# State space output with channels on partitions, and a written order of four engines for groups 2 to 7

## The chip, the cores and the metric

The kernel runs on one core of a Trainium2 chip. Its time is the device time of one execution in microseconds; less is better. The core has TensorE for matrix products (in the profile PE, and PEld for its loading of weights), VectorE (DVE), ScalarE (ACT), GpSimd (POOL) and SyncE (SP), which here issues most of the DMAs that bring the weights in.

## The reference, cut to what matters

The program is one inference step of a streaming encoder: a Mamba-2 mixer, a block of looked-up experts ("peer"), attention, a second peer block and a last norm. The change lies in the mixer, which works on 384 tokens of width 1024: 256 of one prompt and 8 samples of 16 tokens that continue stored states.

```python
def mamba_mixer(xn, ssm_prev, conv_prev, w_in, conv_w, conv_b, dt_bias, a_log, d_skip, norm_g, w_out):
    proj = xn @ w_in
    z, xbc, dt_raw = ...                       # 2048 gates, 2048 x + 1024 B + 1024 C, 32 heads
    xbc, conv_new = causal_conv(xbc, conv_prev, conv_w, conv_b)   # 4 taps in time, then silu
    ...
    dt = softplus(dt_raw + dt_bias)
    y, s_new = ssd_scan(xs, dt, A, Bm, Cm, ssm_prev, ...)
    y = y + xs * d_skip[:, None]               # the skip
    y = y * silu(z)                            # the gate
    y = rmsnorm(y, norm_g)
    return y @ w_out, s_new, conv_new

# in ssd_scan, for each block of tokens i, j, each head r with 64 channels p:
xdt = x * dt
cb = einsum('bcign,bcjgn->bcijg', C, B)
y_diag = einsum('bcijgr,bcjgrp->bcigrp', cb * lmat, xdt)               # inner products
states = einsum('bcjgn,bcjgrp->bcgrpn', B, xdt * decay_end)            # new states
y_off = einsum('bcign,bcgrpn->bcigrp', C, s_prev) * exp(acum)          # products with the old states
y = y_diag + y_off
```

The 32 heads form 8 groups of four; a group shares B and C. A group has 256 channels of x and of z, and 128 each of B and C.

## The kernel before, in words

The tokens lie in three blocks of 128 (NB = 3): two of the prompt and one of all the samples. The normed input is kept with its 1024 features on partitions, split into a high and a low part (xhi, xlo), and so is every weight tile after its load: raw (a DMA of 512 KB on SP's queue), hi (ScalarE, line 132) and lo = raw - hi (VectorE, line 133). A product in full precision is then three matmuls for each of 8 slices of features: hi by xhi, hi by xlo, lo by xhi (lines 168 to 170). 24 such matmuls of 128 columns of weights by 384 tokens are called a tile here.

A group has six pieces of weight: a B tile, a C tile, two x tiles (x0, x1) and two of the gate. The first four end in a convolution (`conv_tile`): GpSimd puts the stored tokens at the head (lines 396, 397), ScalarE evicts the product into xp, GpSimd copies the last tokens out (lines 400, 401), ScalarE makes the first tap, VectorE the other three (line 406), and ScalarE applies silu. These results have channels on partitions. `gate` makes z with tokens on partitions (72 matmuls of 256 columns, lines 460 to 462). `decay` makes ab, a matrix of 128 by 128 tokens for every head and block: the decays (line 473, twelve instructions), an exponential on ScalarE, and the product with C by B (cb). `tokens` transposes x and scales it by dt (xdt) and by dt and the decay to the block's end (xde, line 498).

`states` (line 506) makes the new prompt states. `outputs` computes a group's y with tokens on partitions, in banks of PSUM:

```python
pe.matmul(o[:, j * P:(j + 1) * P], self.xs[:, j, b * P:(b + 1) * P], self.dg[:, j], ...)   # skip, L518
pe.matmul(o[:, cs], self.ab[:, rr, b], self.xdt[:, b, cs], ...)                            # inner, L522
```

Here dg is a diagonal matrix of the skip's weights, which GpSimd makes anew for each group (line 432). The products with the old states (lines 525, 529) stand in a bank of their own, pO; VectorE fades them, adds the rest and multiplies with the gate (lines 534 to 538). ScalarE squares y and sums it over channels into a column of ssq for each block and group. `turn` transposes y (line 547) and splits it into yhi and ylo, the operands of the output projection. `carry` makes the new sample states: it fades s0 (line 553), and eight products (line 561) are added to it.

The program loops over the groups. In loop g stand the tiles of group g and, between them, the steps of the group before: `states` and `outputs` behind the B tile, `turn` behind C, `carry` behind x0. How the instructions come to stand in each engine's queue is decided by a scheduler when the program is built; only where `pin` or `in_order` is used (nowhere in this loop but for the eight products of `carry` and two copies) does the queue keep the order of the code. Group 7's outputs, turn and carry stand in the output projection (`out_terms`, whose sixteen terms are w_out's row blocks). PSUM is used through a ring of eight banks, which are given out in the order of the code.

Of the kernel before, what the change touches and what calls it, by code (L numbers as in the profile page):

```python
# [19 lines left out]
P = 128  # L20
# [48 lines left out]
def encoder_step(ctx: ExitStack, tc: tile.TileContext, t_in, t_out):  # L69
# [165 lines left out]
    def mamba(h_src):  # L235
        with ExitStack() as c:
# [62 lines left out]
            ssq = T(one, [P, NB, GROUPS], F32, tag="ssq")  # L299
# [11 lines left out]
            if True:  # L311
# [77 lines left out]

                def conv_tile(ci, out):  # L390
# [3 lines left out]
                    xp = T(two, [P, XPW], F32, tag="xp")  # L394
                    xs_ = xp[:, PADP:].rearrange("p (s w) -> p s w", w=SEG)
                    pool.memset(xp[:, 0:3], 0.0)
                    pool.tensor_copy(xs_[:, :, 0:3], sconv[:, ci])
                    act.copy(xp[:, 3:PADP], ps[:, :NP])
                    act.copy(xs_[:, :, 3:], ps[:, NP:].rearrange("p (s w) -> p s w", w=TS))
                    pool.tensor_copy(cst[:, ci, 0], xp[:, NP:PADP])  # L400
                    pool.tensor_copy(cst[:, ci, 1:], xs_[:, :, TS:])
                    cv = T(two, [P, XPW], F32, tag="cv")
                    act.activation(cv[:, :CVW], xp[:, 0:CVW], AF.Identity, scale=convw[:, ci, 0:1],
                                   bias=convb[:, ci:ci + 1])
                    for k in range(1, 4):
                        dve.scalar_tensor_tensor(cv[:, :CVW], xp[:, k:k + CVW], convw[:, ci, k:k + 1], cv[:, :CVW],
                                                 op0=OP.mult, op1=OP.add)
                    act.activation(out[:, :NP], cv[:, :NP], AF.Silu)
                    act.activation(out[:, NP:].rearrange("p (s w) -> p s w", w=TS),
                                   cv[:, PADP:].rearrange("p (s w) -> p s w", w=SEG)[:, :, :TS], AF.Silu)  # L410
# [4 lines left out]
                class Group:  # L415


                    def __init__(self, g):
                        self.g = g
                        self.hs = slice(4 * g, 4 * g + 4)  # L420

                    def fetch(self):
                        g = self.g
# [3 lines left out]
                                                        ap=[[0, P], [1, 4 * NB * P]]))  # L427
# [1326 lines left out]
```

## Time and profile before

| what | value |
|---|---|
| time of three runs | 2357.51, 2357.73, 2358.8 us; median 2357.73 |
| the profiled execution | 2358.57 us, its span 2356.7 us, mean granted TensorE clock 0.996 |
| PE, busy share of the span | 2306.2 us, 98% |
| PEld | 1979.3 us, 84% |
| DVE | 1964.8 us, 83% |
| ACT | 1251.5 us, 53% |
| POOL | 764.1 us, 32% |
| the first state product (line 506) of each group | 100.18, 135.68, 171.00, 206.31, 241.62, 277.00 us for groups 1 to 6 |
| start of the output projection | 307.87 us |

Times are in microseconds from the span's start, "xN" counts instructions, and "out<-in" gives the tiles that an instruction writes and reads, with buffer numbers left out. Engines overlap, so their busy times do not add up to the span. The mixer takes the first 387 us or so; the steady part of the loop over groups runs from 100 to 308 us.

### The profile page before, as it was taken

The numbers are of one execution on the slowest core, as the hardware profiler recorded it, in microseconds if no ns is written. First come the engines' busy times: TensorE is split into PE (matmuls) and PEld (weight loads), VectorE is DVE, ScalarE is ACT, GpSimd is POOL, SyncE is SP. The second block draws the span as 40 slices with busy tenths as digits, with TensorE's granted clock in tenths as the row PEclk, the third lists the DMA queues.
The fourth block names the chain that finished last, engine by engine and source line by source line (L and its number), as shares of the span: only waits on it lengthen the run. The fifth ranks groups of instructions, "written<-read, shape, count | busy, mean of one in ns | idle before, by whom it ended". The sixth has DMA issues, their size and how long they took to land. (4 is left out here: it accounts for less than half of the span.)

```text
span 2356.7 us, 44413 instructions
## 1 busy us (share of the span) xinstructions
PE 2306.2 (98%) x16606; PEld 1979.3 (84%) x16607; DVE 1964.8 (83%) x4227; ACT 1251.5 (53%) x2428; POOL 764.1 (32%) x779
## 2 busy tenths in 40 slices
PE   7999999999999999999999999999999999999998
PEld 7899987999999997667776787999999997667775
DVE  5888855979998999888876676979988999898876
ACT  5666534344476676554444555344466666554443
POOL 2323200002154333555563200011144324555562
PEclk9999999999999999999999999999999999999999
DMA  5554435357699889999997515367699889999997
GB/s 189 190 188 170 155 128 185 117 193 246 239 358 334 327 298 333 381 372 387 403 419 295 166 64 181 117 206 258 234 356 333 312 306 334 384 367 391 409 419 282
DMA packets 177944, 649.76 MB, mean 276 GB/s; under 512 B 21232, under 2 KB 23136, under 8 KB 175328
## 3 DMA queue, kind: packets, MB, share of 16 engines
q1 hardware_dynamic: 100800, 365.85, 42.6%
q0 software_dynamic: 76928, 281.07, 31.9%
q8 instruction: 130, 2.13, 0.4%
q14 instruction: 86, 0.70, 0.1%
HBM read 630.62 MB, written 18.06 MB: 275 GB/s over the span
## 5 line engine op out<-in xcount | busy, mean ns | idle before, releaser
L132 ACT CAST hi<-raw 128x1024 fp32r<-128x1024 f32 (+1 forms) x475 | 495.4, 1043 | 666.1 <-PE bank L169 322.6
L133 DVE TENSOR_TENSOR lo<-raw,hi 128x1024 fp32r<-128x1024 f32 (+1 forms) x475 | 575.8, 1212 | 197.7 <-ACT hi L132 196.9
L1250 POOL DMA_INDIRECT gath<-in_p_u,eidU x226 | 288.5, 1276 | 831.7 <-DVE gath L1299 514.9
L168 PE MATMUL bank<-xhi,hi 128*128 128x256 f32 (+1 forms) x1344 | 400.9, 299 | 0.0
L170 PE MATMUL bank<-xhi,lo 128*128 128x256 f32 (+1 forms) x1344 | 393.3, 293 | 5.3 <-DVE lo L133 5.1
L169 PE MATMUL bank<-xlo,hi 128*128 128x256 f32 (+1 forms) x1344 | 392.3, 292 | 0.0
L168 PEld LDWEIGHTS bank<-xhi,hi 128*128 128x128 f32 x1344 | 253.6, 189 | 12.7 <-issue 8.9
L170 PEld LDWEIGHTS bank<-xhi,lo 128*128 128x128 f32 x1344 | 253.3, 188 | 8.2 <-DVE lo L133 8.0
L169 PEld LDWEIGHTS bank<-xlo,hi 128*128 128x128 f32 x1344 | 253.5, 189 | 0.8 <-issue 0.2
L1250 POOL DMA_INDIRECT G<-in_p_v,eidT x192 | 223.8, 1166 | 78.5 <-issue 53.3
L168 PE MATMUL bank<-qhi,hi 128*128 128x256 f32 (+1 forms) x784 | 232.7, 297 | 0.0
L170 PE MATMUL bank<-qhi,lo 128*128 128x256 f32 (+1 forms) x784 | 227.4, 290 | 2.2 <-DVE lo L133 2.2
L169 PE MATMUL bank<-qlo,hi 128*128 128x256 f32 (+1 forms) x784 | 228.4, 291 | 0.0
L1413 ACT ACTIVATE oa<-ioh,e2T 128x128 f16<-128x128 f16 x512 | 163.3, 391 | 96.3 <-PE bank L1425 96.3
L183 PE MATMUL bank<-hi,phi 128*128 128x512 f32 x632 | 206.1, 405 | 1.5 <-ACT phi L132 1.5
L132 ACT CAST hix<-raw 128x1024 fp32r<-128x1024 f32 x118 | 123.9, 1050 | 152.3 <-PE bank L183 69.8
L183 PE MATMUL bank<-lo,phi 128*128 128x512 f32 x632 | 197.7, 392 | 0.9 <-DVE lo L133 0.9
L183 PE MATMUL bank<-hi,plo 128*128 128x512 f32 x632 | 196.4, 390 | 0.0
L133 DVE TENSOR_TENSOR lox<-raw,hix 128x1024 fp32r<-128x1024 f32 x118 | 143.9, 1220 | 22.2 <-ACT hix L132 21.9
L183 PEld LDWEIGHTS bank<-hi,phi 128*128 128x128 f32 x632 | 113.6, 188 | 49.5 <-ACT phi L132 19.1
L170 PEld LDWEIGHTS bank<-qhi,lo 128*128 128x128 f32 x784 | 147.9, 189 | 2.6 <-DVE lo L133 2.6
L169 PEld LDWEIGHTS bank<-qlo,hi 128*128 128x128 f32 x784 | 148.9, 190 | 0.4
(395 smaller groups left out, 5173.1 us busy)
## 6 DMA issues: line engine op xcount, KB each, us to landing
raw<-in_u_t SPq DMA_DIRECT2D x256, 512.0 KB
raw<-in_p_v SPq DMA_DIRECT2D x256, 512.0 KB
raw<-in_w_in SPq DMA_DIRECT2D x32, 512.0 KB
raw<-in_p_w_q SPq DMA_DIRECT2D x32, 512.0 KB
raw<-in_w_z SPq DMA_DIRECT2D x16, 512.0 KB
s<-in_state_ssm SPq DMA_DIRECT2D x8, 1024.0 KB
out_sm_ssm<-s SPq DMA_DIRECT2D x8, 1024.0 KB
raw<-in_w_out SPq DMA_DIRECT2D x16, 512.0 KB
```

The costliest lines, as they stand in the source:

```text
L132: act.copy(hi, raw)
L133: dve.tensor_tensor(lo, raw, hi32, op=OP.subtract)
L168: pe.matmul(ps, whi[:, s], xhi[:, k, c0:c1], start=(k == 0), stop=False)
L169: pe.matmul(ps, whi[:, s], xlo[:, k, c0:c1], start=False, stop=False)
L170: pe.matmul(ps, wlo[:, s], xhi[:, k, c0:c1], start=False, stop=(k == KD - 1))
L183: mm = pe.matmul(halves[hf], x, w[:, hf * n:(hf + 1) * n], start=s_, stop=e_)
L1250: pool.indirect_dma_start(out=tile_, out_offset=None, in_=tab, in_offset=bass.IndirectOffsetOnAxis(ap=idx, axis=0))
L1413: act.activation(a[:, i], ioh, AF.Square, scale=-1.0, bias=e2T[:, t, 0:1])
```

## The change

The mixer's y is now computed with channels on partitions, and the loop is rewritten.

- Inner products: xdt's 64 channels of a head are the stationary operand and ab the moving one, so that a matmul writes 64 partitions by 128 tokens; two heads share a bank, one in its lower and one in its upper half. Skip and gate are applied by VectorE (`gated`), and dg is gone. The gate is two ordinary tiles, with w_z laid out as the other weights are.
- The products with the old states keep their form; faded (yo), they are transposed and added by four matmuls with the identity (`add_outer`).
- y needs no transpose before its split (`turn`). The squares are summed over groups by GpSimd (`squares`), and over channels at the end by three matmuls with a column of ones.
- Groups 0 and 1 are left to the scheduler. For groups 2 to 7 one loop over 36 tiles stands in `in_order` with GpSimd added, so that PE, DVE, ACT and POOL keep the order of the code. Each tile runs its 16 matmuls with high weights and then the 8 with low weights; the raw weights are loaded two tiles ahead; the steps of the group before stand at fixed tiles: its state products inside the B tile, its four new-state pairs (`s0_products`, "four quarters") after x1. The loop also splits the first two blocks of w_out.
- The last `else` of the loop is reached for x0 as well as for z1, so `x_turn` stands twice in a group: behind x0, where its target px is written again later without having been read, and behind z1.

```diff
-                        pY = [bank([P, 256]), bank([P, 2, 256])]
-                        for b in range(NB):
-                            o = pY[0] if b == 0 else pY[1][:, b - 1]
-                            for j in range(2):
-                                pe.matmul(o[:, j * P:(j + 1) * P], self.xs[:, j, b * P:(b + 1) * P], self.dg[:, j],
-                                          start=True, stop=False)
...
+                    def inner(self, j):
+                        self.pY[j] = bank([P, NT])
+                        for b in range(NB):
+                            for r in range(2):
+                                cs = slice(64 * (2 * j + r), 64 * (2 * j + r) + 64)
+                                pe.matmul(self.pY[j][64 * r:64 * r + 64, b * P:(b + 1) * P], self.xdt[:, b, cs],
+                                          self.ab[:, 2 * j + r, b], start=(b == 0), stop=False)
...
-                        dve.tensor_tensor(y[:, 0], self.zs[:, 0], pY[0], op=OP.mult)
-                        dve.tensor_tensor(y[:, 1:], y[:, 1:], pY[1], op=OP.add)
-                        dve.tensor_tensor(y[:, 1:], y[:, 1:], self.zs[:, 1:], op=OP.mult)
-                        for b in range(NB):
-                            act.activation(self.zs[:, b], y[:, b], AF.Square, accum_out=ssq[:, b, g:g + 1])
+                    def add_outer(self):
+                        for j in range(2):
+                            for b in (1, 2):
+                                pe.matmul(self.pY[j][:, b * P:(b + 1) * P], self.yo[:, b - 1, j * P:(j + 1) * P], ident,
+                                          start=False, stop=(b == 2))
...
+                    def gated(self, j):
...
+                        dve.scalar_tensor_tensor(y[:, j], self.xs[:, j], dsk[:, c:c + 1], self.pY[j],
+                                                 op0=OP.mult, op1=OP.add)
+                        dve.tensor_tensor(y[:, j], y[:, j], self.zs[:, j], op=OP.mult)
+
+                    def squares(self, j):
+                        if self.g == 0 and j == 0:
+                            act.activation(ssq, self.y[:, j], AF.Square)
+                        else:
+                            act.activation(self.zs[:, j], self.y[:, j], AF.Square)
+                            pool.tensor_tensor(ssq, ssq, self.zs[:, j], op=OP.add)
...
-                            pt = bank([P, NT])
-                            for b in range(NB):
-                                pe.transpose(pt[:, b * P:(b + 1) * P], self.y[:, b, j * P:(j + 1) * P], ident)
-                            split(yhi[:, ct], ylo[:, ct], pt, scale=ng[:, ct:ct + 1])
+                            split(yhi[:, ct], ylo[:, ct], self.y[:, j], scale=ng[:, ct:ct + 1])
...
+                with in_order(HELD + (mybir.EngineType.Pool,)):
+                    for i, (g, k) in enumerate(tiles):
...
+                        act.copy(nhi, raw)
+                        if pend and pend[0]:
+                            pend[0].evict(pend[2])
+                        elif pend:
+                            act.activation(pend[1], pend[2], AF.Silu)
+                        if k == "b":
+                            if g > 2:
+                                for b in range(NB):
+                                    p.x_scale(b)
+                            p.state_products()
...
+                        if k == "c":
+                            p.state_sum()
+                            p.fade_outer()
+                        dve.tensor_tensor(nlo, raw, nhi.bitcast(F32), op=OP.subtract)
+                        wt = nhi, nlo
+                        if pend and pend[0]:
+                            pend[0].sum()
+                        if k == "b":
+                            c.spans(range(2 if g > 2 else 0, 4))
+                        elif k == "c":
+                            p.s0_fade()
+                        elif k == "x0":
+                            for j in range(2):
+                                p.gated(j)
+                        elif k == "x1":
+                            for j in range(2):
+                                p.squares(j)
+                            p.turn()
+                        elif k == "z0":
+                            p.s0_sum()
+                        elif k == "z1":
+                            p.store()
+                            c.weigh()
+                            if nx:
+                                nx.spans(range(2))
...
+                        if k == "b":
+                            p.inner(0)
+                            p.outer()
+                            p.inner(1)
+                        elif k == "c":
+                            p.add_outer()
+                        elif k == "x1":
+                            p.s0_products(range(4))
+                        elif k == "z0":
+                            c.pairs()
+                            c.b_turn()
+                        else:
+                            for b in range(NB):
+                                c.x_turn(b)
...
-                dve.tensor_reduce(ry, ssq, axis=AX.X, op=OP.add)
-                dve.tensor_scalar(ry, ry, 1.0 / INNER, EPS, op0=OP.mult, op1=OP.add)
+                dve.tensor_scalar(ry, psq[0], 1.0 / INNER, EPS, op0=OP.mult, op1=OP.add)
```

Where the rows stand now is shown at four places (a row is line, operation, tile written, tiles read, shape written). First TensorE's queue at the outputs of one group, before (three more pairs that read like the second one stand behind it and are left out):

```order
L518 MATMUL bank_2336<-dg_1924,xs_2032 128x128
L522 MATMUL bank_2336<-xdt_2259,ab_1920 128x64 x2
L518 MATMUL bank_2337<-dg_1924,xs_2032 128x128
L522 MATMUL bank_2337<-xdt_2259,ab_1920 128x64 x2
L518 MATMUL bank_2337<-dg_1924,xs_2032 128x128
L522 MATMUL bank_2337<-xdt_2259,ab_1920 128x64 x2
L525 MATMUL bank_2356<-st_2329,CT_1972 128x256
L529 MATMUL bank_2356<-s_318_1922,cm_59_252 32x256 x8
```

And the same place now (bank_2513 is the next group's B tile, bank_2593 its C tile):

```order
L704 MATMUL bank_2513<-xlo_108,hi_2478 128x384
L546 MATMUL bank_2545<-xde_2537,Bt_2500 128x256 x2
L724 MATMUL bank_2513<-xhi_107,lo_2479 128x384 x8
L564 MATMUL bank_2569<-ab_1981,xdt_2536 64x128 x6
L569 MATMUL bank_2576<-st_2544,CT_2267 128x256
L573 MATMUL bank_2576<-s_384_2237,cm_61_256 32x256 x8
L564 MATMUL bank_2586<-ab_1981,xdt_2536 64x128 x6
L703 MATMUL bank_2593<-xhi_107,hi_2532 128x384
```

Six skip and twelve inner products became twelve inner products of another shape, and the two state products moved into the B tile, ahead of its eight low-weight matmuls. Next TensorE's queue behind the x0 tile, now:

```order
L704 MATMUL bank_2650<-xlo_108,hi_2614 128x384
L724 MATMUL bank_2650<-xhi_107,lo_2615 128x384 x8
L527 MATMUL bank_2703<-ident_69,xs_2699 128x128 x2
L527 MATMUL bank_2706<-ident_69,xs_2699 128x128 x2
L527 MATMUL bank_2709<-ident_69,xs_2699 128x128 x2
L703 MATMUL bank_2712<-xhi_107,hi_2669 128x384
```

Six transposes of xs stand between x0 and x1, where the queue had none. VectorE's queue from the products with the old states of one group on, before:

```order
L534 TENSOR_TENSOR y_2768<-bank_2758,etok_245 128x512
L553 TENSOR_TENSOR s_378_2324<-s_378_2324,decS_247 128x2048
L537 TENSOR_TENSOR y_2768<-y_2768,bank_2739 128x512
L473 SCALAR_TENSOR_TENSOR ab_3126<-ab_3126,acum_243,msk_251 128x128 x12
L538 TENSOR_TENSOR y_2768<-y_2768,zs_2655 128x512
L133 TENSOR_TENSOR lo_2903<-raw_2900,hi_2902 128x1024
```

And VectorE's queue now, from the gating of a group's y on:

```order
L604 SCALAR_TENSOR_TENSOR y_2690<-xs_2324,dsk_236,bank_2586 128x384
L606 TENSOR_TENSOR y_2690<-y_2690,zs_2450 128x384
L728 TENSOR_TENSOR lo_2734<-raw_2667,hi_2733 128x1024
L414 SCALAR_TENSOR_TENSOR cv_2740<-xp_2700,convw_223,cv_2740 128x408 x3
L136 SCALAR_TENSOR_TENSOR ylo_238<-y_2690,ng_234,yhi_239 128x384 x2
L728 TENSOR_TENSOR lo_2799<-raw_2729,hi_2798 128x1024
L414 SCALAR_TENSOR_TENSOR cv_2805<-xp_2764,convw_223,cv_2805 128x408 x3
```

The twelve decays no longer stand in one piece between two steps of y; a tile's low weights (lo), the convolution of the tile before it and one step of the earlier group follow one another. Last GpSimd's queue, before:

```order
L396 MEMSET xp_1602 128x3
L397 COPY xp_1602<-sconv_227 128x8x3
L400 COPY cst_229<-xp_1504 128x3
L401 COPY cst_229<-xp_1504 128x24
L432 TENSOR_SCALAR dg_1522<-ident_69,dsk_236 128x128 x2
```

And now (zs holds the squares):

```order
L405 COPY cst_229<-xp_1200 128x3
L406 COPY cst_229<-xp_1200 128x24
L613 TENSOR_TENSOR ssq_246<-ssq_246,zs_920 128x384 x2
L398 MEMSET xp_1264 128x3
L399 COPY xp_1264<-sconv_227 128x8x3
```

The two instructions that made dg are gone, and two additions of the squares stand ahead of the memset and copy that open the next convolution.

More of the change, by code (lines that the diff above doesn't have):

```diff
@@ L393, in conv_tile @@
                     gemm_cols(ps, split_raw(early.pop(ci, None) or load_raw(t_in["w_in"][ci])), xhi, xlo, 0, NT)
[L394 to L410, printed above, removed]
+                    t = Conv(ci)
+                    t.evict(ps)
+                    t.sum()
+                    t.silu(out)
                 def heads(ap):
@@ new lines, in b_turn, with b_keep @@
+                    def b_turn(self):
+                        self.pb = bank([P, NB, P])
+                        for b in range(NB):
+                            pe.transpose(self.pb[:, b], self.BT[:, b * P:(b + 1) * P], ident)
+                    def b_keep(self):
+                        self.Bt = Bt = T(two, [P, 4, P], F32, tag="Bt", bufs=1)
+                        act.copy(Bt[:, 0:2], self.pb[:, 0:2])
+                        for w in range(2):
+                            act.activation(Bt[:, 2 + w], self.pb[:, 2], AF.Copy, scale=parm[:, w:w + 1])
@@ L525, in outputs, with outer @@
+                    def outer(self):
+                        self.pO = pO = bank([P, 2, 256])
                         pe.matmul(pO[:, 0], self.CT[:, P:2 * P], self.st[:, 0], start=True, stop=True)
@@ new lines, in mamba @@
+                gs = [Group(g) for g in range(GROUPS)]
+                g0, g1 = gs[:2]
+                st_ = steps()
+                g0.b_tile()
+                g0.c_tile()
+                next(st_)
+                g0.x_tile(0)
+                g0.x_tile(1)
+                g0.gate()
+                next(st_, None)
+                g0.fetch()
+                g0.tokens()
+                g1.b_tile()
+                g1.c_tile()
+                g1.fetch()
+                g1.x_tile(0)
+                g0.decay()
@@ new lines, in mamba, with source @@
+                g0.states()
+                g0.outputs()
+                g1.x_tile(1)
+                g0.finish()
+                g0.carry()
+                g1.decay()
+                g0.turn()
+                g1.gate()
+                g0.store()
+                g1.tokens()
+                tiles = [(g, k) for g in range(2, GROUPS) for k in ("b", "c", "x0", "x1", "z0", "z1")]
+                def source(g, k):
+                    if k[0] == "z":
+                        return t_in["w_z"][g, int(k[1])]
+                    return t_in["w_in"][{"b": 16 + g, "c": 24 + g, "x0": 2 * g, "x1": 2 * g + 1}[k]]
@@ L625, in out_terms @@
                         elif ct == 9:
+                            psq.append(bank([P, NB]))
+                            for b in range(NB):
+                                pe.matmul(psq[0][:, b:b + 1], ssq[:, b * P:(b + 1) * P], ones1[:, 0:1], start=True, stop=True)
                             last.store()
                             sync.dma_start(t_out["convs"], cst)
-                        yield (load_split(t_in["w_out"][ct * P:(ct + 1) * P, :]),
+                        yield (ready[ct] if ct < 2 else load_split(t_in["w_out"][ct * P:(ct + 1) * P, :]),
                                lambda b, ct=ct: yhi[:, ct, b * P:(b + 1) * P],
```

295 lines of the change are left out of this document (180 added, 115 removed).

## The prediction

> **What bounds the kernel now.** I read first the busy time of each engine by stages, with edges set at the first state product of each group (line 506), since that comes once a group; then what TensorE waits for in that stretch; then the timeline of TensorE through one group. The columns after the stretch and its length are busy microseconds and, in brackets, instructions of PE, PEld, DVE, ACT and POOL, then the granted clock, the DMA share and GB/s. Below them stands the only TensorE wait between 100 and 308 us.
>
> ```profile
> 100.18:135.68 35.50, 35.50 (x263) 33.64 (x264) 30.83 (x54) 20.19 (x43) 9.58 (x20) 1.00 0.53 202
> ...
> 206.31:241.62 35.31, 35.31 (x265) 33.44 (x265) 29.74 (x50) 21.22 (x44) 10.82 (x20) 1.00 0.50 176
> ...
> 277.00:307.87 30.87, 30.87 (x241) 29.17 (x240) 23.66 (x31) 15.80 (x40) 6.93 (x16) 1.00 0.43 147
> PE bank L506 <- DVE xde L498: 0.7, 1, 0.7
> ```
>
> TensorE is busy for all of a group's 35.31 us at full clock and waits for nothing in the steady groups, while VectorE has 5.57 us to spare. So a microsecond of TensorE work taken out of a group is a microsecond of the program, as long as VectorE, which the change loads further, does not take its place. Everything behind the output projection keeps its order of instructions on all five queues, but for two neighbouring VectorE rows that change places; I let it move as a block and cost it at nothing, since what starts it, the end of the projection, is TensorE work too.
>
> Now TensorE's timeline through one group; what an instruction costs is the step from its start to the next start, since the durations overlap. xN counts records; a plain fp32 matmul leaves two.
>
> ```profile
> 181.68 0.38 PE L547 MATMUL bank<-ident,y 128*128 128x128 f32 x2
> 181.82 0.42 PE L168 MATMUL bank<-xhi,hi 128*128 128x384 f32 x1
> ...
> 187.24 0.66 PE L547 MATMUL bank<-ident,y 128*128 128x128 f32 x4
> 187.65 0.42 PE L168 MATMUL bank<-xhi,hi 128*128 128x384 f32 x1
> ...
> 192.81 0.36 PE L460 MATMUL bank<-hi,xhi 128*128 128x256 f32 x1
> ...
> 197.49 0.49 PE L496 MATMUL bank<-ident,xs 128*128 128x128 f32 x3
> 197.95 0.39 PE L461 MATMUL bank<-lo,xhi 128*128 128x256 f32 x1
> ...
> 201.82 0.49 PE L496 MATMUL bank<-ident,xs 128*128 128x128 f32 x3
> 202.06 0.42 PE L168 MATMUL bank<-xhi,hi 128*128 128x384 f32 x1
> ...
> 206.31 0.59 PE L506 MATMUL bank<-xde,Bt 128*128 128x256 f32 x2
> 206.74 0.39 PE L518 MATMUL bank<-dg,xs 128*128 128x128 f32 x2
> 206.96 0.60 PE L506 MATMUL bank<-xde,Bt 128*128 128x256 f32 x2
> 207.40 0.56 PE L522 MATMUL bank<-xdt,ab 128*128 128x64 f32 x4
> ...
> 211.14 0.65 PE L525 MATMUL bank<-st,CT 128*128 128x256 f32 x2
> 211.72 1.07 PE L529 MATMUL bank<-s,cm 128*32 128x256 f32 x16
> 212.72 0.44 PE L168 MATMUL bank<-xhi,hi 128*128 128x384 f32 x1
> 213.00 0.33 PE L169 MATMUL bank<-xlo,hi 128*128 128x384 f32 x1
> ```
>
> **The change, part by part (a minus is time saved in a group).**
>
> *Outputs.* The block from 206.31 to 212.72 is 6.41 us: four records of state products (0.43 + 0.44 = 0.87), 36 records of skip (dg) and inner products (206.74 to 206.96 and 207.40 to 211.14, that is 3.96, or 0.11 a record), and 1.58 of products with the old states (211.14 to 212.72). The new block has the state products, two runs of 12 records for the inner products and the same 1.58. The new inner product writes 64 channels, so its weights are 64 columns wide, 128 tokens pass through, and neighbouring matmuls write the lower and the upper half of the partitions. The trace has that very form in the attention, in runs of 8 and of 16 records:
>
> ```profile
> 1348.65 0.66 PE L866 MATMUL bank<-pT,kv 128*64 128x128 f32 x8
> 1349.24 0.44 PE L168 MATMUL bank<-xhi,hi 128*128 128x384 f32 x1
> ...
> 1355.30 1.09 PE L866 MATMUL bank<-pT,kv 128*64 128x128 f32 x16
> 1356.32 0.39 PE L795 MATMUL bank<-maskS,idb 128*128 128x512 bf16 x1
> ```
>
> Eight take 0.59 and sixteen 1.02, so twelve take 0.81, and two such runs 1.61. The state products now stand inside the B tile, which costs one more return to a 384-wide matmul: the step after a return is 0.28 (212.72 to 213.00) where a record of a tile takes 4.25/24 = 0.18, so +0.11. New block: 0.87 + 0.11 + 1.61 + 1.58 = 4.17; change -2.24. The bounds of the inner part are 1.02 for a run, as if twelve cost what sixteen do (+0.4 for both), and 24 times 0.11 if the halves do not overlap here, a rival below.
>
> *Transposes of y* go: 0.14 (181.68 to 181.82) and 0.41 (187.24 to 187.65), with a return saved: -0.64. *Add of the outer part*, four full fp32 matmuls with the identity, 8 records at 0.11 and a return: +0.97. *Gate:* 72 matmuls of 256 from 192.81 to 202.06 less the 0.46 and 0.24 of the transposes between them are 8.55; the two new tiles cost what a conv tile does, 202.06 to 206.31 = 4.25 each: -0.05. *Transposes of x* stand together, 6 at 0.08 (0.24 for three): 0.48 against 0.70, -0.22. But the branch that holds them is the loop's last "else", so it also runs in x0's place, where xs has just been allocated; those six results are overwritten and only cost: 0.48 + 0.09 = +0.57. *Tiles in two passes* (16 matmuls with the high weights, then 8 with the low) are the same 24: 0.
>
> Sum for a group: -2.24 - 0.64 + 0.97 - 0.05 - 0.22 + 0.57 = -1.61, so 33.70 us, and -9.7 over the six groups 2 to 7. Group 0's outputs, outside the written order, have neither the second return nor the useless transposes: -2.24 - 0.11 - 0.64 + 0.97 = -2.0. Group 7's, in the projection, I take as -1.8, since there they break up the projection's matmuls. The sums of squares become six records with one column at 0.08: +0.5. Together -13.0 of TensorE work. The first splits of w_out made ahead I cost at 0: 307.87 follows without a gap already.
>
> *VectorE, GpSimd and the new order.* What VectorE and GpSimd do in a group:
>
> ```profile
> L406 DVE SCALAR_TENSOR_TENSOR cv<-xp,convw,cv 128x408 f32<-128x408 f32 x12 | 7.7, 642 | 0.8 <-ACT cv L403 0.6
> L133 DVE TENSOR_TENSOR lo<-raw,hi 128x1024 fp32r<-128x1024 f32 x6 | 7.3, 1222 | 2.8 <-ACT hi L132 2.8
> L473 DVE SCALAR_TENSOR_TENSOR ab<-ab,acum,msk 128x128 f32<-128x128 f32 x12 | 3.2, 347 | 0.0
> ...
> L136 DVE SCALAR_TENSOR_TENSOR ylo<-bank,ng,yhi 128x384 fp32r<-128x384 f32 x2 | 1.1, 612 | 0.0
> ...
> L538 DVE TENSOR_TENSOR y<-y,zs 128x512 f32<-128x512 f32 x1 | 0.7, 685 | 0.0
> L537 DVE TENSOR_TENSOR y<-y,bank 128x512 f32<-128x512 f32 x1 | 0.7, 680 | 0.0
> ...
> L536 DVE TENSOR_TENSOR y<-zs,bank 128x256 f32<-128x256 f32 x1 | 0.4, 417 | 0.0
> ...
> L432 POOL TENSOR_SCALAR dg<-ident,dsk 128x128 f32<-128x128 f32 x16 | 12.4, 783 | 16.8 <-PE bank L518 16.8
> ...
> L444 POOL COPY cm<-CT 128x64 f32<-128x64 f32 x16 | 4.4, 302 | 8.1 <-ACT CT L409 8.1
> ```
>
> VectorE loses 1.8 (lines 536 to 538) and gains four operations of 384, at the 1.1 a pair of line 136: 29.74 + 0.4 = 30.1 of 33.7 us. The order written out makes one stretch of it count: from the fading of the old-state products (their end lies 0.8 before the end of the B block, behind which the second inner run stands) to the second xde, which TensorE now waits for in the middle of the next B tile, two thirds of 4.25 = 2.8 in. Between lie the other five blocks, 33.7 less the B block's 8.4 (4.25 + 4.17): 0.8 + 25.3 + 2.8 = 28.9 us. VectorE's work in it is 30.1 less what stands outside, a split (1.2), half the decays (1.6) and about 1.4 of state sum and last x scale: 25.9; with a wait for ScalarE's eviction of x1 (0.6, the wait in line 406's row) 2.4 us are left over.
>
> Into that stretch come two GpSimd additions of 128x384 for the squares, in front of the memset and copy that x1's convolution waits for. What they cost no row shows. GpSimd and VectorE get in each other's way:
>
> ```profile
> 216.26 3.23 DVE L473 SCALAR_TENSOR_TENSOR ab<-ab,acum,msk 128x128 f32<-128x128 f32 x12
> 219.41 0.69 DVE L538 TENSOR_TENSOR y<-y,zs 128x512 f32<-128x512 f32 x1
> 220.01 1.22 DVE L133 TENSOR_TENSOR lo<-raw,hi 128x1024 fp32r<-128x1024 f32 x1
> ...
> 212.47 0.20 POOL L397 COPY xp<-sconv 128x24 f32<-128x24 f32 x1
> ...
> 218.39 2.89 POOL L400 COPY cst<-xp 128x3 f32<-128x3 f32 x1 [5.72 <-ACT xp L398]
> ```
>
> A copy of three elements lasts 2.89 us, to 221.28, beside VectorE operations with both inputs in SBUF that run to 221.23. This rule speaks against the change: the Trainium skill, page "SBUF — State Buffer", section "Who interferes with whom", says that such a VectorE operation and a GpSimd one that reads SBUF exclude each other for a whole instruction, whichever came first. By that rule the trace agrees, and each addition would also hold VectorE up for its length.
>
> Let X be the length of an addition. If both hold VectorE up in full, TensorE stands 2X - 2.4 a group. From below X is 0.3, the copy of 64 elements (line 444); from above three times line 432, 2.35, and the stall 2.3. The copies grow from 0.20 at 24 elements to 0.30 at 64, 0.0025 each, which makes 1.1 at 384 and no stall; I take that, for it reads and writes as an addition does, and add 0.4 a group for work that finds the other engine in its way where the count of slack is coarse (six tile ends, each with some 0.1 of hand-over): +2.4. The Trainium skill, page "GPSIMD Engine Reference", section "Elementwise — side-by-side cycle accounting", has 4497 ns for an addition of 2048 elements; an estimate by that page is 0.84 for 384, and the sum would be -13.0, no stall.
>
> Sum: -13.0 + 2.4 = -10.6. The profiled execution took 2358.57 (span 2356.7 and 1.9 around it), 0.84 above the median of 2357.73; from the median the time is 2347.1 us.
>
> **Rivals.** *No stall at all*: 2357.7 - 13.0 = 2344.7; for it speaks the 2.4 us of slack, against it that VectorE is then busy 30.1 of 33.7 and its order can no longer give way. *The two halves do not overlap*: +2.64 - 1.61 = 1.03 a group with outputs, eight of them, +8.2; the longer group gives VectorE slack, so no stall: -4.8, 2352.9. Against it stands line 866, the same shape. *VectorE late at the state products (the slower side)*: the additions last so long that xde comes after two thirds of the B tile; TensorE stands there since the products are ahead of the low-weight matmuls. It decides from 6(2X - 2.4) = 13.0, X = 2.3; at X = 2.9, additions that wait as long as the copy at 218.39, it is 6 x 3.4 - 13.0 = +7.4, 2365.1. For it speaks that row, against it that between the three dependent operations of a convolution GpSimd finds gaps. *The written order only moves the waits*: a cost of 1.5 to 2.2 a group from ScalarE or bank hand-over, 2353 to 2358, no change; for it speaks that eight banks go round 22 times a group.
>
> **How the numbers follow.** About 0.2%, 4.7 us, is what a measurement of this kernel can tell from no change: faster is below 2353.0, slower above 2362.4. Forecast 2345.5 to 2351: 0.55. No stall, below 2345.5: 0.15. Halves apart or a stall up to 1.4 a group, 2351 to 2353: 0.09. Order moves the waits, within 0.2%: 0.15. VectorE late, slower: 0.06. So faster 0.79, same 0.15, slower 0.06. The range runs from 2343.5, no stall and a microsecond found in groups 0 and 1, to 2355.0, which takes in the halves apart and a part of the moved waits, and leaves some 0.17 out.
>
> **What will show it.** Right: the step from state products to state products is 33.5 to 34.5 us; each inner run of twelve 0.8; TensorE waits for xde in the middle of the B tile 0 to 0.5 a group; the additions about 1.1. Wrong: a TensorE wait above 2 a group on xde, lo or a bank; inner runs of 1.3; additions above 2; or a gain beyond 387 us, which I do not expect.

## The result, and the profile after

The changed kernel took 2344.37 us (median of 8 runs, 2340.64 to 2352.62) against 2359.8 us for the kernel before (8 runs on the same chip): ratio 0.9944, 95% interval 0.9928 to 0.9960. Timed a second time on another chip it took 2349.3 against 2359.18, ratio 0.9951 (0.9938 to 0.9964). So it is faster by some 0.5%. 2347.1 us had been forecast, and both times lie in the range. On the forecast's base of 2357.73 us the two ratios are 2344.5 and 2346.2: the first lies just inside the band "no stall, below 2345.5", which had a chance of 0.15, the second in the band that had 0.55.

First the stretches of the mixer, cut at the first state product of a group, with the columns of the table shown for the kernel before, and below them the only wait of TensorE between 100 and 308 us:

```profile
97.83:132.50 34.67, 33.92 (x237) 31.34 (x236) 32.48 (x55) 20.61 (x39) 10.30 (x20) 1.00 0.57 215
132.50:166.51 34.01, 34.01 (x236) 31.39 (x236) 31.91 (x52) 20.84 (x39) 10.31 (x20) 1.00 0.52 184
166.51:200.47 33.96, 33.96 (x236) 31.34 (x236) 31.87 (x52) 20.84 (x39) 10.32 (x20) 1.00 0.53 182
...
268.39:299.49 31.10, 31.10 (x220) 28.56 (x220) 29.00 (x43) 20.71 (x39) 9.74 (x18) 1.00 0.44 159
PE bank L546 <- DVE xde L534: 0.7, 1, 0.7
```

A steady group takes 33.96 us instead of 35.31 (34.1 was forecast), with TensorE listed as busy throughout. VectorE now stands at 31.87 of 33.96, ScalarE and GpSimd are as busy as before. Then TensorE's timeline through one group and at two later marks:

```profile
200.47 1.23 PE L546 MATMUL bank<-xde,Bt 128*128 128x256 f32 x4
201.35 1.74 PE L724 MATMUL bank<-xhi,lo 128*128 128x384 f32 x8
203.02 0.88 PE L564 MATMUL bank<-ab,xdt 128*64 128x128 f32 x12
203.83 0.70 PE L569 MATMUL bank<-st,CT 128*128 128x256 f32 x2
204.46 1.07 PE L573 MATMUL bank<-s,cm 128*32 128x256 f32 x16
205.46 0.88 PE L564 MATMUL bank<-ab,xdt 128*64 128x128 f32 x12
206.26 0.44 PE L703 MATMUL bank<-xhi,hi 128*128 128x384 f32 x1
...
210.53 1.05 PE L597 MATMUL bank<-ident,yo 128*128 128x128 f32 x8
211.34 0.42 PE L703 MATMUL bank<-xhi,hi 128*128 128x384 f32 x1
...
215.59 0.82 PE L527 MATMUL bank<-ident,xs 128*128 128x128 f32 x6
216.16 0.42 PE L703 MATMUL bank<-xhi,hi 128*128 128x384 f32 x1
...
299.49 0.71 PE L183 MATMUL bank<-hi,yhi 128*128 128x512 f32 x2
...
1338.40 0.66 PE L1049 MATMUL bank<-pT,kv 128*64 128x128 f32 x8
```

The two inner runs are 0.81 and 0.80 us (0.81 forecast), the products with the old states 1.63, the add of the outer part 0.81, the useless transposes behind x0 0.57. The output projection starts 8.4 us earlier than before (299.49 against 307.87), the first product behind the mixer 9.7 us earlier (line 1044 before, 1227 now, 389.91 and 380.23), and the first product with pT in the attention 10.25 us earlier (1338.40 against 1348.65). Behind that, in code that did not change, the lead moves between 6.0 and 10.3 us, and the spans differ by 8.4. One reason is seen in this execution: TensorE's granted clock is 0.93 from 1400 to 1450 us (the third number from the end), 1.00 in the profile before, shown behind it, and over this stretch the lead shrinks from 10.2 to 7.6.

```profile
1400.00:1450.00 50.00, 45.38 (x321) 37.33 (x315) 31.28 (x52) 27.65 (x58) 1.65 (x3) 0.93 0.42 142
...
1400.00:1450.00 50.00, 45.21 (x370) 35.64 (x369) 31.51 (x58) 25.01 (x60) 1.65 (x3) 1.00 0.47 161
```

Why a group is not shorter than 33.96 us is seen on VectorE, ScalarE and GpSimd. The rows follow one another in time:

```profile
204.35 1.49 ACT L493 ACTIVATE ab<-ab 128x1536 f32<-128x1536 f32 x1 [0.94 <-DVE ab L489]
205.59 0.69 DVE L579 TENSOR_TENSOR yo<-bank,etok 128x512 f32<-128x512 f32 x1 [0.42 <-PE bank L573]
205.74 1.03 ACT L713 CAST hi<-raw 128x1024 fp32r<-128x1024 f32 x1
206.80 1.23 DVE L728 TENSOR_TENSOR lo<-raw,hi 128x1024 fp32r<-128x1024 f32 x1 [0.52 <-ACT hi L713]
...
218.61 3.25 DVE L414 SCALAR_TENSOR_TENSOR cv<-xp,convw,cv 128x408 f32<-128x408 f32 x3
218.71 2.70 POOL L613 TENSOR_TENSOR ssq<-ssq,zs 128x384 f32<-128x384 f32 x2
221.95 0.42 ACT L418 ACTIVATE xs<-cv 128x256 f32<-128x256 f32 x1 [1.93 <-DVE cv L414]
222.48 1.03 ACT L713 CAST hi<-raw 128x1024 fp32r<-128x1024 f32 x1
223.54 1.23 DVE L728 TENSOR_TENSOR lo<-raw,hi 128x1024 fp32r<-128x1024 f32 x1 [0.62 <-ACT hi L713]
```

Twice in a group VectorE waits for ScalarE's cast of the next weights (hi), which stands in ScalarE's queue behind work that itself waits for VectorE: the exponential of the decays (ab) and the silu of x0 (xs). With VectorE's own work between these points this closes a ring through VectorE and ScalarE: a chain of steps that leads back to itself one group later, so that its length bounds the group. VectorE also waits 0.42 for TensorE's products with the old states; which of the two waits belongs to the ring these rows do not tell (e5 does). And the convolution of x0 takes 3.25 us instead of the 2.00 of the others, while two GpSimd additions run beside it (e7 shows that they are the cause). This loss of VectorE's is called the hold below.

### The profile page after: what moved, and what is told of

The parts are those of the page before. It is cut to its first block, busy times and chain, and to the rows that moved or that the text cites. A ratio compares the mean times of both kernels' runs of the same rounds, so it can differ in the third digit from the quotient of the medians.

```text
span 2348.3 us, 43951 instructions
## 1 busy us (share of the span) xinstructions
PE 2299.7 (98%) x16376; PEld 1965.5 (84%) x16377; DVE 1979.3 (84%) x4234; ACT 1246.7 (53%) x2388; POOL 764.7 (33%) x779
## 5 line engine op out<-in xcount | busy, mean ns | idle before, releaser
L132 ACT CAST hi<-raw 128x1024 fp32r<-128x1024 f32 (+1 forms) x439 | 457.8, 1043 | 615.8 <-PE bank L169 280.8
L133 DVE TENSOR_TENSOR lo<-raw,hi 128x1024 fp32r<-128x1024 f32 (+1 forms) x439 | 531.0, 1210 | 182.1 <-ACT hi L132 181.6
L168 PE MATMUL bank<-xhi,hi 128*128 128x256 f32 (+1 forms) x1184 | 344.8, 291 | 1.3 <-ACT hi L132 1.3
L170 PE MATMUL bank<-xhi,lo 128*128 128x256 f32 (+1 forms) x1184 | 338.9, 286 | 3.6 <-DVE lo L133 3.6
L169 PE MATMUL bank<-xlo,hi 128*128 128x256 f32 (+1 forms) x1184 | 338.0, 285 | 0.0
L168 PEld LDWEIGHTS bank<-xhi,hi 128*128 128x128 f32 x1184 | 223.2, 189 | 11.3 <-issue 5.9
L170 PEld LDWEIGHTS bank<-xhi,lo 128*128 128x128 f32 x1184 | 222.7, 188 | 6.5 <-DVE lo L133 6.0
L169 PEld LDWEIGHTS bank<-xlo,hi 128*128 128x128 f32 x1184 | 223.1, 188 | 0.8 <-issue 0.2
```

The costliest lines, as they stand in the source:

```text
L132: act.copy(hi, raw)
L133: dve.tensor_tensor(lo, raw, hi32, op=OP.subtract)
L168: pe.matmul(ps, whi[:, s], xhi[:, k, c0:c1], start=(k == 0), stop=False)
L169: pe.matmul(ps, whi[:, s], xlo[:, k, c0:c1], start=False, stop=False)
L170: pe.matmul(ps, wlo[:, s], xhi[:, k, c0:c1], start=False, stop=(k == KD - 1))
```

## The experiments

Seen as a sum over five steps from the first state product of one group to that of the sixth (five groups), from the start of each line to its end: 100.18 to 277.00, 176.8 us before; 97.83 to 268.39, 170.6 us for the changed kernel. The experiments are compared by this and by the step of a steady group, from its first state product to the next group's, which repeats within 0.02 us where the order is written out. The groups 2 to 7 are called the written groups.

**e1, the useless transposes out.**

```diff
-                        else:
+                        elif k == "z1":
                             for b in range(NB):
                                 c.x_turn(b)
```

> The changed kernel with the second x_turn taken out (the branch is made to hold for z1 alone). TensorE-bound: the step from state products to state products falls from 33.96 by the 0.57 us of the six transposes and the 0.09 by which the x1 tile was longer than x0 (4.34 against 4.25), to 33.3; five steady groups and the last make -3.3 to -4.0 us against the changed kernel. The wait for xde in the second written group, 0.75 us, grows to 1.4. Rival, VectorE already the bound: a wait for xde of 0.3 or more appears in every group, and less than half of the 0.66 is gained.

Time 2349.97 against 2361.35, ratio 0.9949 (0.9937 to 0.9962): not told apart from the changed kernel. The step is 33.90, only 0.06 less, and TensorE now waits in every group:

```profile
197.97 1.27 PE L546 MATMUL bank<-xde,Bt 128*128 128x256 f32 x4 [0.38 <-DVE xde L534]
```

The rival held: 0.66 us of TensorE work had gone and nearly all of it came back as waiting for VectorE. The changed kernel stands on the edge between TensorE's work and the other engines.

**e2, the new arithmetic alone.** The loop of the kernel before, order left to the scheduler, around the new steps:

```diff
                         prev.states()
                         prev.outputs()
                     G_.c_tile()
...
                     if g > 1:
+                        prev.finish()
                         prev.turn()
```

> The new form of the outputs, gate, squares and skip in the loop of the kernel before, with the order left to the scheduler; no written order, no second x_turn, state products behind the whole B tile. If the gain is in the arithmetic: TensorE work of a group is the changed kernel's 33.96 less 0.66 for the useless transposes and 0.28 for the return inside the B tile, 33.0, so the program is 5 us faster than the changed kernel, some 15 to 18 below the kernel before. If the written order is needed: the scheduler's queues leave TensorE waits of 1 us or more in a group for VectorE (32 of 33 us busy), and the period is 34 or more, no faster than the changed kernel.

Time 2369.32 against 2361.35, ratio 1.0035 (1.0021 to 1.0049): slower than the kernel before. One group, then five groups together, and TensorE's largest wait from 100 to 313 us (what is waited for, us in all, times, longest):

```profile
143.01:178.47 35.46, 34.01 (x230) 30.59 (x230) 30.02 (x51) 20.71 (x39) 10.16 (x20) 1.00 0.48 174
101.57:284.44 182.87, 171.43 (x1147) 154.40 (x1147) 151.43 (x255) 103.80 (x195) 49.64 (x100) 0.98 0.49 178
PE bank L499 <- ACT CT L418: 10.3, 5, 6.3
```

In the one group TensorE is busy for 34.0 of 35.46 us, 1.0 more than expected; most of the rest is the wait of the product of C and B for C's silu on ScalarE. The five groups take 182.9 us, 6.1 more than before. The first of them alone takes 41.4, with a wait of 6.3 us and a granted clock of 0.92; the other four average 35.36, against 35.33 before. So the arithmetic alone gains nothing, with that one group or without it: in the scheduler's order TensorE's own work shrinks less than expected, and waiting takes the rest.

**e3, the halves one after the other.**

```diff
-                        for b in range(NB):
-                            for r in range(2):
+                        for r in range(2):
+                            for b in range(NB):
```

> The changed kernel with the inner products of one bank in another order: three blocks of the lower half of the partitions, then three of the upper half, instead of alternating. If neighbouring matmuls on the two halves overlap and that makes 0.067 us a record, each run of twelve goes from 0.81 to about 1.2 (up to 12 times 0.11 = 1.3) and the period grows by 0.8 to 1.0. If the small tile alone makes the rate, the runs stay at 0.81 and the period at 33.96.

One run, 2351.93 us; the step is 34.30.

```profile
202.90 1.14 PE L564 MATMUL bank<-ab,xdt 128*64 128x128 f32 x12
203.97 0.70 PE L569 MATMUL bank<-st,CT 128*128 128x256 f32 x2
```

A run of twelve takes 1.07 instead of 0.81. So alternating the halves does shorten a run, but not all of the difference to the 0.11 a record of the kernel before hangs on it: 0.089 one half after the other, 0.067 alternating. The group grew by 0.34, less than the 0.5 of two runs and the 0.8 to 1.0 expected, since the 0.21 of waiting inside the state products (below) went with it.

**e4, four more GpSimd additions.**

```diff
                             p.store()
+                            for j in range(2):
+                                for _ in range(2):
+                                    pool.tensor_tensor(p.y[:, j], ssq, p.y[:, j], op=OP.add)
                             c.weigh()
```

> The changed kernel with four more GpSimd additions of 128x384 per group, in z1's place, into a tile that is read no more (the outputs do not change). In the changed kernel each addition beside VectorE's convolution lasts 1.3 us and makes VectorE's operation twice as long, +0.63 each. Theory: GpSimd's additions hold VectorE up; four more cost VectorE 2.5 us in the stretch to xde, the slack left there is about 1.1 (2.4 by the prediction's count less 1.25 for the two additions), so TensorE waits about 1.4 us for xde in each steady group, period 35.3. Rival, VectorE is not held up in general: no wait, period 33.96, and VectorE's operations beside the additions keep their lengths.

One run, 2352.34 us. The step is 35.22 and TensorE waits 1.05 for xde. VectorE and GpSimd at the place, each of the four additions and each operation of the convolution by itself; x4 is four instructions:

```profile
229.83 0.65 DVE L414 SCALAR_TENSOR_TENSOR cv<-xp,convw,cv 128x408 f32<-128x408 f32 x1
229.94 1.40 POOL L749 TENSOR_TENSOR y<-ssq,y 128x384 f32<-128x384 f32 x1
230.51 1.27 DVE L414 SCALAR_TENSOR_TENSOR cv<-xp,convw,cv 128x408 f32<-128x408 f32 x1
231.42 1.24 POOL L749 TENSOR_TENSOR y<-ssq,y 128x384 f32<-128x384 f32 x1
231.82 1.28 DVE L414 SCALAR_TENSOR_TENSOR cv<-xp,convw,cv 128x408 f32<-128x408 f32 x1
232.62 1.36 POOL L749 TENSOR_TENSOR y<-ssq,y 128x384 f32<-128x384 f32 x1
234.06 1.02 POOL L749 TENSOR_TENSOR y<-ssq,y 128x384 f32<-128x384 f32 x1
...
233.02 2.46 DVE L643 TENSOR_TENSOR s<-s,bank 128x512 f32<-128x512 f32 x4
240.67 1.27 PE L546 MATMUL bank<-xde,Bt 128*128 128x256 f32 x4 [1.05 <-DVE xde L534]
```

Two additions lay beside the convolution, whose inputs are both in SBUF: each made one of its operations last 1.27 instead of 0.65. The third began while the last of these operations ran and took 1.36, the fourth 1.02. Beside the sum of new states (line 643, one input in PSUM) they cost VectorE nothing: 2.46, as in the changed kernel (2.47). The step grew by 1.26, two times 0.63. The expected step of 35.3 was met by two errors that cancel: the hold was 1.26, not 2.5, because two of the four additions fell mainly beside operations that they do not hold up, and none of the supposed slack of 1.1 was left. By the rule of the Trainium skill, page "SBUF — State Buffer", section "Who interferes with whom", a VectorE instruction with at most one input in SBUF does not contend with GpSimd, outside the modes in which it takes both ports, and one with two does where the GpSimd instruction reads SBUF. The trace agrees on both.

**e5, state products behind the B tile** (on top of e1).

```diff
                         if k == "b":
                             if g > 2:
                                 for b in range(NB):
                                     p.x_scale(b)
-                            p.state_products()
                         for kk in range(KD):
                             pe.matmul(ps, wlo[:, kk * P:(kk + 1) * P], xhi[:, kk], start=False, stop=(kk == KD - 1))
+                        if k == "b":
+                            p.state_products()
```

> The changed kernel without the second x_turn, as e1, and with the state products moved from the middle of the B tile to its end. Theory: with the useless transposes out, a ring bounds the groups: old-state products end on TensorE, VectorE's chain to the second xde (28.9 us), back to TensorE (5.0 us from the first state product through 8 low-weight matmuls, inner run and old-state products), 33.9 in all. Behind the tile the path on TensorE is 3.3 instead of 5.0, the ring 32.2, and TensorE's work is the bound again: 33.9 less the 0.38 wait and the 0.28 of the return, about 33.2 a group, no wait for xde in the steady groups; 4 us below e1, and the new states' place inside the B tile costs time. Rival: VectorE's sum of work is the bound, not the ring; then the wait for xde stays 0.3 or more wherever the products stand, and the time is e1's.

Time 2347.03 against 2359.18, ratio 0.9944 (0.9930 to 0.9959), beside e6 on the same chip: not told apart from it. The step stayed 33.91 and the wait stayed:

```profile
200.42 1.27 PE L546 MATMUL bank<-xde,Bt 128*128 128x256 f32 x4 [0.41 <-DVE xde L534]
...
206.80 1.23 DVE L729 TENSOR_TENSOR lo<-raw,hi 128x1024 fp32r<-128x1024 f32 x1 [1.03 <-ACT hi L713]
```

My theory fell: a ring through TensorE would have opened. VectorE no longer waits for the old-state products (0.42 in e1), but 1.03 instead of 0.52 for the cast on ScalarE, and the sum is much the same (1.03 and 0.94). So the wait for TensorE does not belong to the ring. The rival written down before the run came out as it said, but VectorE's work alone does not fill the step: it is busy for 31.79 of the 33.91 us, and most of the rest are its waits for ScalarE's cast (1.03 and 0.57). So the ring is read as running through ScalarE's queue, as in the rows of the profile after; no run moved ScalarE's work to test that by itself. e7 and e11 test what follows for VectorE.

**e6, the changed kernel again**, with no edit.

> The changed kernel itself, unedited, timed beside the others on this chip: by the trace it should be 9 to 10 us below the kernel before at equal granted clock, 0.4% (the mixer ends 9.4 us earlier), against the 13 of the first comparison. e1 should be no more than 3 us below it.

Ratio 0.9951 (0.9938 to 0.9964), 9.9 us by the medians; the steps are the same to 0.01 us (33.96, 33.97). The gain of the first trace up to the attention, 10.25 us, lies in both intervals. This run's own trace has less: 8.05 us at the projection's start (299.82), 9.4 at the first product behind the mixer (380.55), 8.2 at the attention (1340.46). So behind the mixer the lead scatters by 2 us between executions of one kernel.

**e7, additions on VectorE** (on top of e1).

```diff
-                            pool.tensor_tensor(ssq, ssq, self.zs[:, j], op=OP.add)
+                            dve.tensor_tensor(ssq, ssq, self.zs[:, j], op=OP.add)
```

> e1 with the two additions of squares on VectorE in place of GpSimd. Theory: GpSimd's two additions hold VectorE's convolution up by 1.25 us; on VectorE they cost two steps of about 0.5. The ring shortens by 0.2 to 0.3: period 33.9 to 33.65, the wait for xde 0.38 to 0.1, and the convolution of x0 is 2.0 us again instead of 3.25. Rival, GpSimd does not hold VectorE up (the convolution is long for another reason): the convolution stays 3.25 and the period grows by 1.

One run, 2350.52 us, with a mean clock of 0.992; the step is 33.10 and no TensorE wait is left in the groups.

```profile
196.00 1.02 PE L546 MATMUL bank<-xde,Bt 128*128 128x256 f32 x4
196.67 1.74 PE L724 MATMUL bank<-xhi,lo 128*128 128x384 f32 x8
...
213.54 2.00 DVE L414 SCALAR_TENSOR_TENSOR cv<-xp,convw,cv 128x408 f32<-128x408 f32 x3
215.45 1.21 DVE L613 TENSOR_TENSOR ssq<-ssq,zs 128x384 f32<-128x384 f32 x2
216.58 1.14 DVE L136 SCALAR_TENSOR_TENSOR ylo<-y,ng,yhi 128x384 fp32r<-128x384 f32 x2
217.64 1.22 DVE L728 TENSOR_TENSOR lo<-raw,hi 128x1024 fp32r<-128x1024 f32 x1
```

The convolution is back at 2.00, so the additions were what held it, and the two additions cost 1.13 on VectorE (215.45 to 216.58). That much I expected, and a step of 33.65 with it. I had not seen that they now lie where VectorE had waited 0.57 to 0.62 for the cast: that wait is gone too. 1.25 + 0.6 - 1.13 = 0.7, against 0.80 by which the step fell; by VectorE's work alone it could have fallen by 0.12 only. At 33.10 TensorE's work is the bound, so the ring is no longer than that. Moving work onto the busier of the two engines shortened its ring.

**e9, the same kernel timed.**

> The kernel of e7 (additions of squares on VectorE, no second x_turn), timed. Its trace had a period of 33.10 with no wait for xde, and the output projection began 7.1 us earlier than in the changed kernel (292.44 against 299.49). At equal granted clock it should be 6 to 7 us below the changed kernel and 16 to 18 below the kernel before: ratio 0.992 to 0.993 to before. If the gain is lost again behind the mixer, the ratio stays at 0.995.

2345.72 against 2358.67, ratio 0.9944 (0.9932 to 0.9957). The trace kept its promise (step 33.10, projection at 292.22, 7.3 us ahead of the changed kernel), the times did not show the full ratio: it is below the changed kernel's two measurements by 0 to 0.0007, with intervals some 0.003 wide. The granted clock can account for the difference. Over the 76 timed runs on record, kernel by kernel and chip by chip, a thousandth of mean granted clock goes with some 1.7 us. e9's runs had a median of 0.992, those of the kernel before beside it 0.995, an estimated 5 us, which takes the 13 measured to 18, where 16 to 18 had been expected at equal clock. Whether this kernel itself brings the clock down no run shows; e10 below, with the same step, had 0.993 to 0.996. So e9 is faster than the changed kernel by the traces and, by this estimate, at equal clock; the times as measured do not tell them apart.

**e10, additions on VectorE and state products behind the tile**, the edits of e5 and e7 together.

> The kernel of e9 with the state products behind the B tile, as in e5. The groups are now bound by TensorE's work, so the return inside the B tile (1.67 for eight low-weight matmuls that take 1.39 elsewhere) should show: period 33.10 less 0.28, up to 0.1 more where the next run follows fp32 matmuls, so 32.8 to 32.9, and 1.2 to 1.8 us for the program. If xde or the old states' eviction is late there, a wait of 0.2 or more appears and the gain is gone.

2342.45 against 2358.67, ratio 0.9929 (0.9915 to 0.9942), the fastest version tried; its interval overlaps e9's. In the trace the move gives nothing, the step is 33.10 again:

```profile
197.23 1.02 PE L546 MATMUL bank<-xde,Bt 128*128 128x256 f32 x4
198.18 0.88 PE L564 MATMUL bank<-ab,xdt 128*64 128x128 f32 x12
```

The state products take 0.95 here and 0.67 inside the tile, where the low-weight matmuls behind them take 1.67 instead of 1.39. In both places the 0.28 is paid to what follows the state products, and the expected 32.8 to 32.9 fell.

**e11, additions on VectorE alone**, useless transposes left in.

> The changed kernel with the additions of squares on VectorE and nothing else; the useless transposes stay. If the two engines' ring (VectorE, ScalarE's exponential and cast, VectorE) was what hid the transposes in e1, the period is 33.10 plus their 0.57 and the return, 33.75, the state products take 0.67 instead of 0.88, and there is no wait in the second written group. If the ring does not matter, the period is 33.96 or longer.

One run, 2354.58 us (mean clock 0.991). The step is 33.76, there is no wait in the second written group, and the state products take 0.67:

```profile
198.77 1.02 PE L546 MATMUL bank<-xde,Bt 128*128 128x256 f32 x4
199.44 1.74 PE L724 MATMUL bank<-xhi,lo 128*128 128x384 f32 x8
```

As expected to 0.01. So the changed kernel's 33.96 are 33.75 of TensorE work and 0.21 of trailing behind xde inside the state products (0.88 instead of 0.67), which no wait row shows. The four steps fit together: 33.96 as changed, 33.90 without the transposes (e1), 33.76 without the hold (e11), 33.10 without both (e7, e9). The transposes cost 0.66 once VectorE is out of the way and 0.06 while it is not.

**e8, the order left free.**

```diff
-                with in_order(HELD + (mybir.EngineType.Pool,)):
+                with in_order(()):
                     for i, (g, k) in enumerate(tiles):
```

> The changed kernel with its loop as written, but with no engine held to the order of the code: the scheduler decides, as in the kernel before. If the order of the code alone is enough, the period is 33.9 to 34.5. If the written order is needed: TensorE waits of 1 us or more a group, as in e2, and a period of 35 or more.

One run, 2361.45 us. Over five groups and the waits from 100 to 307 us:

```profile
100.64:276.87 176.23, 172.30 (x1177) 156.48 (x1177) 155.63 (x258) 105.62 (x195) 48.32 (x100) 1.00 0.51 180
PE bank L527 <- ACT xs L418: 2.4, 2, 1.4
```

Five groups take 176.2 us, as before the change (176.8), against 170.6 with the order held. 2.5 of the 5.7 are TensorE's own (172.3 busy against 169.8 in the same five steps), the rest are waits, 0.8 a group where 1 or more had been expected. In these groups the code in its new sequence is worth next to nothing unless the queues keep it.

## Why the prediction was right, step by step

**The work.** Forecast 33.70 us a group, measured 33.75. The block of outputs, counted as in the prediction, is 4.19 in e11 (0.67 + 0.28 + 0.81 + 1.63 + 0.80) against 4.17; in it the return inside the B tile was mis-sized (0.28, not 0.11) and the state products as well (0.67 for the four together, not 0.87). The add of the outer part was a little dear (0.81 and a return, against 0.97), the useless transposes a little cheap (0.66, against 0.57).

**The stall.** Forecast 0.4 a group, measured 0.21: near, but not for the reason given. The price X of an addition was right: 1.1 taken, 1.02 with nothing in its way and 1.3 beside the convolution. That each holds VectorE up for its whole length was wrong: 0.63 each. The slack of 2.4 us was wrong the other way: the hold of 1.25 leaves a stall of 0.21, so there was about 1.0. The count let the stretch from the fading to the second xde depend on TensorE's old-state products, with a single wait of 0.6 for ScalarE in it; the runs showed a second wait of ScalarE's cast behind the exponential of ab, and the ring that it closes. The count itself gave no stall (2.2 of hold in 2.4 of slack); the 0.4 was a margin put on top, with no row behind it. That a hold and a slack that were both too large nearly cancelled, and that the margin came near 0.21, is luck. The case named for the slower side, VectorE late at the state products, is real as a mechanism: e4 has it, with 1.05 a group, and so has the 0.7 us in the second written group: in the group ahead of it twelve decays stand in place of six.

**Where the sum came out.** Over the five steps the forecast was 5 times -1.21, -6.0; measured 176.8 to 170.6, -6.3. From the projection's start to the first product behind the mixer -1.3 was forecast (group 7's -1.8 and +0.5) and -1.3 measured (9.7 less 8.4, and 9.4 less 8.05 in e6). The -2.0 for group 0 is seen in half at most: what is left of the 8.4 up to the projection is -2.1, where group 0's -2.0 and one more group's -1.2 were counted. At the start of group 2's B tile nothing of it is seen: 94.95 us in the changed kernel, 92.7 to 95.4 in its variants whose order is written out, 94.17 before. From 30 us to there TensorE's two largest waits are 1.4 for st and 1.3 for hi in the changed kernel, 1.2 for Bt and 1.0 for st before; what became of the missing microsecond stays open. In all it is -9.7 at the end of the mixer (-9.4 in e6) against -10.6 forecast. The run's ratios, -0.56% and -0.49%, are -13.2 and -11.6 of 2357.73. The median granted clock was 0.997 in the first measurement of the changed kernel and 0.9935 in the second, which at 1.7 us a thousandth (e9) covers the whole difference of its two medians, 2344.37 and 2349.3. In the second the kernel before had 0.995 beside it, so that at equal clock the gain would be an estimated 12 us, some 3 more than the mixer's. A gain beyond 387 us was named as a sign of being wrong. Whether there is one is not settled, since in the traces the lead behind the mixer scatters by more than that.

**The rivals.** That the halves do not overlap fell with the runs of 0.81, and e3 shows what one half after the other costs: 0.34 a group. That the written order only moves the waits fell too, and e2 and e8 turn it round: without the order there is no gain, and the new arithmetic in the old loop is 0.35% slower than the kernel before. The prediction had put the gain down to arithmetic and charged the order with a loss. The old arithmetic in a written order was not run; in the kernel before TensorE had no waits in the steady groups that an order could have taken away, so the gain most likely needs both.

## What to carry to other kernels

When an engine is listed as busy all the time, look whether its small groups take longer than elsewhere: 0.88 against 0.67 was a stall without a wait row, and told that another ring sat on the same length. Follow a ring through every queue, ScalarE's too, before calling a sum of idle time slack: here a wait for a cast that stood behind an exponential was not slack. Judge work that seems useless, and work that seems harmless on an idle engine, together: taking out one alone gained 0.06 or 0.20 us a group, both together 0.86. And compare the granted clocks before calling two times equal.

## What the runs showed of the hardware

- A GpSimd addition of 128x384 in fp32 took 1.02 us beside VectorE operations with a PSUM input and 1.2 to 1.4 beside a VectorE operation with two SBUF inputs, which went from 0.65 to 1.27. Per addition VectorE lost 0.63, less than the addition's own length: in e4 an addition that began while a VectorE operation ran was itself the longer one (1.40 and 1.36), so the delay goes both ways. The estimate by the page "GPSIMD Engine Reference" of the Trainium skill, 0.84 for 384 elements from its 4497 ns for 2048 (section "Elementwise — side-by-side cycle accounting"), is below the 1.02 measured; a cost that does not shrink with the length would explain it, and no run here separates it.
- fp32 matmuls with 64 columns of weights and 128 tokens took 0.067 us a record when neighbours write different halves of the partitions, and 0.089 when three follow one another in the same half.
